# Output projection block by block, plain operands in other rows, x1 stored in halves: one change to a hybrid decoder block on one core

## The chip, the core and the metric

The kernel runs on one core of a Trainium2 chip. Time is device time in microseconds (us) of one execution. The profile is one execution recorded by the hardware profiler, and its engines are PE (TensorE, matmuls; PEld its weight loads), DVE (VectorE), ACT (ScalarE), POOL (GpSimd) and SP (SyncE, which here only issues DMAs). "PEclk" is the share of full speed that the throttle granted to TensorE.

## The reference

A decoder block on x of 1024 tokens by 1024 channels, fp32: an input projection, two token mixers (A: gated chunks, B: dilated windowed attention), and then

```python
gates = jax.nn.sigmoid(gate_logits.reshape(b, s, N_BRANCHES, D_MODEL))
merged = gates[:, :, 0] * (y_a @ w_branch_a[layer]) + gates[:, :, 1] * (y_b @ w_branch_b[layer])
x = x + merged @ w_out[layer]
h2 = rms_norm(x, ffn_norm_g[layer])
up = h2 @ w_up[layer]
a, val = up[..., :D_FF], up[..., D_FF:]
a = causal_depthwise_conv(a, conv_w[layer], conv_b[layer])
x = x + (jax.nn.gelu(a, approximate=False) * val) @ w_down[layer]
```

and a final RMSNorm. D_FF is 2816, handled as 22 units of 128 columns (`ff` = 0 to 21). The change touches the span from the gating of the last branch tiles to the first units of `h2 @ w_up`.

## The kernel before

**Products.** Every large product is a 2x2 Strassen-Winograd scheme: seven products P1 to P7 of half-size operands with sums before and after them. Each is done in three passes of rounded fp32 parts (hi by hi, hi by lo, lo by hi). `to_parts` makes an operand: ACT copies the source into the hi part (L165), DVE or POOL subtracts it from the source for the lo part (L166). A 128x512 output tile is one bank of PSUM; three pools hold them: `acc` (3 banks), `dn` (3 banks) and `tr` (2 banks).

**What sets the order.** PE follows the order of the program throughout. From `write_order()` on, during the last branch tiles, until the last product of unit 1 (P3), DVE and ACT follow the order of the program too; the order is written out by hand there, down to single operations: `to_parts` puts its lo subtraction on a list, and `low(n)` emits the next n of them. POOL and SP, and what the program makes behind that stretch, go where a scheduler puts them, and a tile's buffer or row of SBUF can be reused once all its readers are done.

**Branch merge** (L1205, L1304 to L1309). Per channel tile `dt` and token half `h`, PE makes `pa` and `pb`, ACT takes the sigmoid of the gates `g` (L1304; for `dt` 6 and 7 just before the use), and DVE multiplies and adds. `pa` sits in an `acc` bank, `pb` in a `dn` bank.

**Output projection** (`out_step`, L1555; `out_result`; the large loop over `OSEQ`). The products come in the order P1, P2, P6, P5, P3, P7, P4, each of four token blocks `blk` and four contraction tiles `kt`, so 12 matmuls of 512 columns a block. P2 adds into the banks of P1, P3 into those of P5, P4 into those of P7. Blocks 0 to 2 of P1 and P5 are in `acc` banks, block 3 in a `tr` bank. P1 runs `kt` outermost: the first tile of all four blocks, then the second. The other products run block by block. `out_ops` are the operands from `w_out` (`out_op`), the first three in a tile called `lead`. After a block of P3 (tokens 0 to 511) or P4 (tokens 512 to 1023) its 1024 channels are complete: ACT squares and sums the last half (`square_h`, L1503), SP stores the row block to `x1d` in DRAM (in `norm_h`, L1511, 512 KB), POOL makes the scale in three small operations (`finish_rms`, L2023 and L2028), ACT and DVE scale a half each (`scale_h`, L1516 and L1517), PE transposes (`turn_h`, L1462), and DVE writes the transposed block over the old one in `Y` (L1466). So L1466 must wait until the store of that block has read `Y`.

**Beginning of the up projection** (`beginning_up`). Unit 0 is a plain product in four pieces (`plain_product_up`, `pu`, L1701) with operands `plain_up[which, k]` in the rows R13, R14, R15 and opx0 of SBUF. They are made at P4: `(0,0)` and `(0,1)` of `up_0_0` ahead of P4's first block, `(1,0)` and `(1,1)` of `up_1_0` behind its first two blocks. Units 1 and 2 run as `up_product` (L1722): P1 and P2 of unit 1, P1 and P2 of unit 2, then the second tokens' half of the plain unit (`pu_1_0`, `pu_1_1`), then P6, P7, P5, P4, P3 of unit 1. ACT copies P1 out (`t1`, L1735) before P2 may add into the same bank; P4 adds into the bank of P7 after DVE has read it (`v`, L1743). `sums_h` (L1816 to L1819) makes the sums of the second operand on DVE, `taps` (L1657 on ACT, then L1659 on DVE) the convolution. In between DVE makes the lows of the operands A21, A22, S2, S3, S1, S4.

The lines that matter most for the change:

```python
if name == "P1":
    out_step(accs[m], name, s, m)
else:
    out_step(accs[n], name, 4 * j + m, n)
...
plain_rows = {(0, 0): (R, 13), (0, 1): (R, 14), (1, 0): (R, 15), (1, 1): (opx, 0)}
lead_rows = {(1, "P1"): (opx, 1), (1, "P2"): (opx, 2), (2, "P1"): (opx, 3), (2, "P2"): (R, 12)}
```

## Time and profile before

| | |
|---|---|
| median of three runs | 1428.24 us (1427.3 to 1428.31) |
| the profiled execution's own time | 1428.74 us |
| its span | 1427.0 us |
| PE busy | 1392.2 us, 98% of the span |
| DVE, ACT, POOL busy | 71%, 46%, 21% |
| mean granted clock | 0.991 |

The span has four large stages by the lines that PE runs: the input projection and attention to about 585 us, the branch merge to 673 us, the output projection from there to 765 us, the up projection to about 1200 us, and the down projection to the end. The change lies between 660 and 830 us. A row of the timeline gives the start, the duration, the engine, the line and the tiles (out<-in), and in brackets how long the engine had been idle before it and whose result it waited for. A row of windows gives, for a stretch of time, the busy time of each engine, the granted clock and the share of the DMA engines.

### The profile page before, as it was taken

The page shows a single profiled execution, that of the slowest core. Times are in us where ns is not written, and L with a number is a line of the kernel's source. Part 1 is how long each engine was busy: PE and PEld are TensorE (multiplying, and loading weights), DVE is VectorE, ACT ScalarE, POOL GpSimd, SP SyncE. Part 2 cuts the span into 40 slices and gives each one's busy share as a digit, 9 for nine tenths or more (in the row PEclk, how much of TensorE's full clock was granted, in tenths as well). Part 3 has the DMA queues.
Part 4 walks back from the last instruction along what each step waited for, and adds up shares of the span by engine and source line. Part 5 has one row for each costly group of instructions (what it writes and reads, how often), then busy time and mean ns, then how long its engine had stood idle before and what let it go on. Part 6 is the DMA issues. An engine that isn't in the chain of part 4 may idle for free.

```text
span 1427.0 us, 19428 instructions
## 1 busy us (share of the span) xinstructions
PE 1392.2 (98%) x6534; PEld 1149.2 (81%) x6534; DVE 1007.8 (71%) x1887; ACT 650.9 (46%) x1266; POOL 298.7 (21%) x296
## 2 busy tenths in 40 slices
PE   8899999999999999999999899999999999999997
PEld 7777788888888888887887678888888887888886
DVE  7877677676886987768787866556556557676674
ACT  5554255555553333533545533333333435354453
POOL 0002000000231000111001165555655543000002
PEclk9999999999999999999999999999999999999999
DMA  6013636354435996793742122223333227986663
GB/s 238 15 48 104 192 85 181 98 175 133 134 111 192 338 311 226 231 300 117 250 150 96 45 103 90 80 89 118 119 119 117 85 95 242 360 317 240 199 205 118
DMA packets 140340, 230.73 MB, mean 162 GB/s; under 512 B 13392, under 2 KB 57168, under 8 KB 140240
## 3 DMA queue, kind: packets, MB, share of 16 engines
q1 hardware_dynamic: 138800, 227.33, 47.9%
q10 hardware_dynamic: 1440, 2.16, 0.4%
q8 instruction: 51, 0.84, 0.2%
q14 instruction: 49, 0.40, 0.1%
HBM read 163.57 MB, written 64.29 MB: 160 GB/s over the span
## 4 chain that ended last, share of the span: by engine, by line
PE 83%; DVE 9%; issue 3%; ACT 2%; POOL 1%; DMA 1%; SPq 0%; POOLq 0%; DVEq 0%; ACTq 0%
PE in_P L491 27%; PE uP L1722 19%; PE dn L1923 12%; PE up L1722 7%; PE wo_P L1555 4%; PE pa L1205 3%; PE pu L833 2%; PE pl L552 2%; DVE R L166 1%; PE pp L817 1%; PE pb L1205 1%; PE warm L344 1%; PE sc L778 1%; PE sc L779 1%; DVE G L166 1%
## 5 line engine op out<-in xcount | busy, mean ns | idle before, releaser
L491 PE MATMUL in_P<-R,G 128*128 128x512 f32 x1008 | 243.7, 394 | 0.0
L491 PEld LDWEIGHTS in_P<-R,G 128*128 128x128 f32 x1008 | 185.6, 188 | 36.8
L1923 PE MATMUL dn<-R 128*128 128x512 f32 x924 | 209.6, 389 | 0.0
L1923 PEld LDWEIGHTS dn<-R 128*128 128x128 f32 x924 | 173.4, 188 | 36.0
L1722 PE MATMUL uP<-R,opx 128*128 128x512 f32 x756 | 183.6, 396 | 0.6 <-POOL opx L166 0.6
L1722 PEld LDWEIGHTS uP<-R,opx 128*128 128x128 f32 x756 | 142.6, 189 | 34.7 <-POOL opx L166 1.0
L165 ACT ACTIVATE G<-wr 128x512 fp32r<-128x512 f32 x126 | 79.1, 630 | 151.2 <-PE in_P L491 114.9
L1722 PE MATMUL uP<-G,opx 128*128 128x512 f32 x504 | 126.7, 401 | 5.2 <-DVE Y L1743 4.8
L491 PE MATMUL in_P<-G,G 128*128 128x512 f32 x504 | 122.7, 394 | 1.0 <-DVE C L518 1.0
L1722 PEld LDWEIGHTS uP<-G,opx 128*128 128x128 f32 x504 | 96.3, 192 | 28.8 <-issue 3.6
L165 ACT ACTIVATE opx<-up 128x512 fp32r<-128x512 f32 x88 | 55.5, 632 | 130.6 <-DVE up L278 55.7
L1722 PE MATMUL up<-G,R 128*128 128x512 f32 x468 | 113.1, 390 | 0.7 <-ACT t L1735 0.7
L491 PEld LDWEIGHTS in_P<-G,G 128*128 128x128 f32 x504 | 92.8, 188 | 19.8 <-ACT G L165 1.2
L1722 PEld LDWEIGHTS up<-G,R 128*128 128x128 f32 x468 | 87.9, 188 | 20.1 <-ACT t L1735 1.1
L166 DVE TENSOR_TENSOR G<-wr,G 128x512 fp32r<-128x512 f32 x126 | 87.8, 698 | 21.7 <-ACT G L165 21.6
L165 ACT ACTIVATE R<-db 128x512 fp32r<-128x512 f32 x77 | 48.3, 629 | 68.1 <-PE dn L1923 53.8
L166 DVE TENSOR_TENSOR R<-db,R 128x512 fp32r<-128x512 f32 x77 | 53.7, 701 | 27.9 <-ACT R L165 27.8
L491 PE MATMUL in_P<-G 128*128 128x512 f32 x252 | 62.2, 393 | 0.0
L884 POOL TENSOR_TENSOR ld<-ld,w 128x256 f32<-128x256 f32 x16 | 11.2, 721 | 236.5 <-DVE w L872 236.5
L1751 POOL TENSOR_TENSOR Y<-Y 128x512 f32<-128x512 f32 x21 | 32.2, 1534 | 132.7 <-ACT Y L1654 132.7
L166 POOL TENSOR_TENSOR wbl<-wbs,wbh 128x512 fp32r<-128x512 f32 x12 | 16.0, 1348 | 199.9 <-DMA gated<-C 139.0
L166 POOL TENSOR_TENSOR opx<-up,opx 128x512 fp32r<-128x512 f32 x40 | 56.7, 1417 | 0.0
(283 smaller groups left out, 2516.4 us busy)
## 6 DMA issues: line engine op xcount, KB each, us to landing
wr<-in_w_in_dram SPq DMA_DIRECT2D x46, 512.0 KB, 4.0
up<-in_w_up_dram SPq DMA_DIRECT2D x44, 512.0 KB, 4.2
dA<-gd SPq DMA_DIRECT2D x55, 256.0 KB, 5.0
wd<-in_w_down_dram SPq DMA_DIRECT2D x44, 256.0 KB, 5.2
wT<-wd SPq DMA_DIRECT2D x44, 256.0 KB, 4.0
dS<-gS SPq DMA_DIRECT2D x44, 256.0 KB, 4.2
db<-wT SPq DMA_DIRECT2D x44, 256.0 KB, 4.6
gd<-Y SPq DMA_DIRECT2D x42, 256.0 KB, 2.0
```

What stands on the lines that cost most here:

```text
L165: nc.scalar.activation(hi, src, AF.Copy)
L166: fn = lambda: lo_eng.tensor_tensor(lo, src, f32(hi), ALU.subtract)
L344: nc.tensor.matmul(warm[:, :P], ident, ident, start=True, stop=True)
L491: nc.tensor.matmul(acc, op[:, w, kt, :], left[LEFT[name], kt][:, a, :], start=opened and kt == 0 and i == 0, stop=kt == QK - 1 and i == 2, ...
L552: nc.tensor.matmul(acc, plain_ops[n, k, i][:, w, kt, :], left[f"A{h + 1}{k + 1}", kt][:, a, :], start=k == 0 and kt == 0 and p == 0, stop= ...
L778: nc.tensor.matmul(dst, self.qa[:, h, :], keys, start=True, stop=False)
L833: nc.tensor.matmul(pu[:, h * HD : (h + 1) * HD], self.pT[:, i, :], vt[:, h * HD : (h + 1) * HD], start=i % n == 0, stop=i % n == n - 1,)
L1205: nc.tensor.matmul(acc, unit[a][kt // 4][:, kt % 4, :], two(R, 8 * h + kt)[:, b, :], start=n == 0 and i == 0, stop=n == len(kts) - 1 and i ...
L1555: nc.tensor.matmul(acc, left[LEFT[name], kt][:, a, blk * P : (blk + 1) * P], out_ops[s][:, w, :], start=name not in SHARED and kt == 0 and ...
L1722: nc.tensor.matmul(acc, op[:, w, kt, :], left[LEFT[name], kt][:, a, :], start=opened and kt == 0 and i == 0, stop=kt == QK - 1 and i == 2, ...
L1751: nc.gpsimd.tensor_tensor(ge1, ge1, v, ALU.mult)
L1923: nc.tensor.matmul(accs[blk], dops[s][:, 0, a, blk * P : (blk + 1) * P], dops[s][:, 1, w, :], start=SEQ[j] not in CONTINUES and kt == 0 an ...
```

## The change

1. **P1 of the output projection runs block by block** like the others. Its first three blocks are copied out (L1523, ACT) after the third block, the fourth after itself.
2. **Gates.** `gate_b` is split: `gate_load` issues the two loads, `sigmoid` the activation. For `dt` 6 and 7 each stands on its own line now, the sigmoid one product or more ahead of the `merge` that uses it; the sums, the operands of `w_out` (`out_op`) and the lows between the last four merges are reordered.
3. **The plain unit's operands** move to the rows R4 to R7 and are made behind blocks 2 and 3 of P7. Their sources are loaded from the end of P3. Their lows stand behind the first result of P4.
4. **x1 is stored in halves**: `square_h` stores the half that it squares (256 KB), `norm_h` stores nothing. For the blocks 4 to 7 the transposed lower half goes to `s3` (a part of the tile `own`) instead of over the old one, and `sums_h`, A21 and S3 read it there.
5. **Leads regrouped**: P1 of unit 1, P1 of unit 2, P2 of unit 1, P2 of unit 2, for the making of operands and on PE.
6. **Taps split** into `begin_taps` (ACT) and `end_taps` (DVE), with other work of the two engines between them; S3's parts are made ahead of the taps of units 1 and 2, and `pu_1_1` runs ahead of the making of S1's parts.

How the instructions stand, at three places (`wo_P7_1` is the PSUM bank of P7 and P4, block 1; the trailing number only tells one tile from another). PE at the beginning of the first product, before:

```order
L1555 MATMUL wo_P1_0_6169<-lead_5423,G0_77 128x512 x3
L1555 MATMUL wo_P1_1_6170<-lead_5423,G0_77 128x512 x3
L1555 MATMUL wo_P1_2_6171<-lead_5423,G0_77 128x512 x3
L1555 MATMUL wo_P1_3_6172<-lead_5423,G0_77 128x512 x3
L1555 MATMUL wo_P1_0_6169<-lead_5423,G0_77 128x512 x3
```

and after the change:

```order
L1565 MATMUL wo_P1_0_6169<-lead_5423,G0_77 128x512 x9
L1565 MATMUL wo_P1_0_6169<-R_75,G0_77 128x512 x3
L1565 MATMUL wo_P1_1_6170<-lead_5423,G0_77 128x512 x9
L1565 MATMUL wo_P1_1_6170<-R_75,G0_77 128x512 x3
L1565 MATMUL wo_P1_2_6171<-lead_5423,G0_77 128x512 x9
```

The bank of block 2 is first written after 6 matmuls before, and after 24 now; the fourth operand (`R_75`) is first read after 36 matmuls before, and after 9 now.

DVE around the end of P7 and the beginning of P4, before (L1541 adds P7's result, L1546 P4's; the `up_` rows are the lows of the plain unit's operands; L1517 scales, L1466 writes the transposed halves):

```order
L1541 TENSOR_TENSOR Y_5416<-Y_5416,wo_P7_3_6609 128x512
L166 TENSOR_TENSOR R_75<-up_0_0_6684,R_75 128x512 x2
L1546 TENSOR_TENSOR Y_5416<-Y_5416,wo_P7_0_6606 128x512
L166 TENSOR_TENSOR R_75<-up_1_0_6686,R_75 128x512
L1546 TENSOR_TENSOR Y_5416<-Y_5416,wo_P7_1_6607 128x512
L1517 TENSOR_SCALAR xn_4_1_6772<-Y_5416,fr_n2_4_6748 128x512
L1466 TENSOR_TENSOR Y_5416<-ht_4_0_6789,chan_80 128x512
L1466 TENSOR_TENSOR Y_5416<-ht_4_1_6795,chan_80 128x512
```

and after the change (L1551, L1556, L1527 and L1475 are the same lines by their new numbers):

```order
L1551 TENSOR_TENSOR Y_5416<-Y_5416,wo_P7_3_6617 128x512
L1556 TENSOR_TENSOR Y_5416<-Y_5416,wo_P7_0_6614 128x512
L166 TENSOR_TENSOR R_75<-up_0_0_6610,R_75 128x512 x2
L1556 TENSOR_TENSOR Y_5416<-Y_5416,wo_P7_1_6615 128x512
L1527 TENSOR_SCALAR xn_4_1_6780<-Y_5416,fr_n2_4_6762 128x512
L166 TENSOR_TENSOR R_75<-up_1_0_6612,R_75 128x512
L1475 TENSOR_TENSOR own_6241<-ht_4_0_6797,chan_80 128x512
L1475 TENSOR_TENSOR Y_5416<-ht_4_1_6803,chan_80 128x512
```

The first result of P4 stands ahead of the two lows of `up_0_0` now, and the first low of `up_1_0` behind the scaling of block 4; the lower transposed half goes to `own`.

ACT from the scaling of block 7 on, before (the four rows `R_75<-Y_5416` are the hi parts of A21, `G1_76<-Y_5416` those of A22, then of S2; `t1` is the copy of a P1):

```order
L1516 ACTIVATE xn_7_0_6884<-Y_5416,fr_n2_7_6854 128x512
L165 ACTIVATE R_75<-Y_5416 128x512 x4
L1657 ACTIVATE own_6241<-pu_0_0_6857,chan_80 128x512
L165 ACTIVATE G1_76<-Y_5416 128x512 x4
L1826 ACT_TABLE_LOAD
L1826 ACTIVATE own_6241<-own_6241 128x512
L165 ACTIVATE opx_6155<-up_0_2_6752 128x512
L165 ACTIVATE R_75<-up_0_2_6752 128x512
L1735 ACTIVATE t1_1_6980<-up_1_6967 128x512
L1735 ACTIVATE t1_2_7017<-up_2_7004 128x512
L165 ACTIVATE G1_76<-Y_5416 128x512 x4
L1657 ACTIVATE Y_5416<-up_1_6967,chan_80 128x512
```

and after the change:

```order
L1526 ACTIVATE xn_7_0_6892<-Y_5416,fr_n2_7_6862 128x512
L165 ACTIVATE R_75<-up_0_3_7175 128x512
L165 ACTIVATE R_75<-own_6241 128x512 x4
L1663 ACTIVATE own_6241<-pu_0_0_6865,chan_80 128x512
L165 ACTIVATE G1_76<-Y_5416 128x512 x4
L1835 ACT_TABLE_LOAD
L1835 ACTIVATE own_6241<-own_6241 128x512
L165 ACTIVATE opx_6155<-up_0_1_6694 128x512
L165 ACTIVATE R_75<-up_0_2_6716 128x512
L1743 ACTIVATE t1_1_6988<-up_1_6975 128x512
L1743 ACTIVATE t1_2_7003<-up_2_6990 128x512
L165 ACTIVATE G1_76<-Y_5416 128x512 x4
```

The hi part of unit 3's P2 operand, from `up_0_3`, stands directly behind the scaling of block 7 and ahead of A21's parts; before, the same operation came 15 rows further down. Its lo part has moved likewise on DVE, from behind the first result of unit 1's P6 to ahead of the transposed block 7. No line of the diff says so: the program makes this operand behind the stretch written out by hand, the scheduler may put it ahead, and the row R14 that it writes no longer holds an operand of the plain unit. It waits for the load of `up_0_3`, which in turn waits for the second low of `up_1_0`, whose buffer it takes.

The diff, cut to its core (the reordered calls of the merges are shown by their first half):

```diff
+    def gate_load(dt, h):
+        t = gates[dt, h] = wp.tile([P, 2, HALF], F32, name=f"g_{dt}_{h}", tag="gt", bufs=3)
+        for br in range(2):
+            nc.sync.dma_start(t[:, br, :], gated[br, dt, :, h * HALF : (h + 1) * HALF])
+    def sigmoid(dt, h):
+        nc.scalar.activation(gates[dt, h], gates[dt, h], AF.Sigmoid)
     def gate_b(dt):
-        if dt < KT:
-            for h in range(2) if dt < KT - 1 else (1, 0):
-                t = wp.tile([P, 2, HALF], F32, name=f"g_{dt}_{h}", tag="gt", bufs=3)
-                for br in range(2):
-                    nc.sync.dma_start(t[:, br, :], gated[br, dt, :, h * HALF : (h + 1) * HALF])
-                if dt < LAST_B:
-                    nc.scalar.activation(t, t, AF.Sigmoid)
-                gates[dt, h] = t
+        for h in range(2):
+            gate_load(dt, h)
+            if dt < LAST_B:
+                sigmoid(dt, h)
...
         gt = gates[dt, h]
-        if dt >= LAST_B:
-            nc.scalar.activation(gt, gt, AF.Sigmoid)
         nc.vector.tensor_tensor(gt[:, 0, :], gt[:, 0, :], pa, ALU.mult)
...
     last_b = write_order()
-    sums_and_parts(1)
     prep_b(KT - 1)
+    sigmoid(KT - 2, 0)
     for q in range(2):
...
         out_load(q, st.rearrange("p (k a) c -> p k (a c)", k=2))
+    gate_load(KT - 1, 1)
+    sums_and_parts(1)
+    out_op(0)
+    out_op(1)
+    sigmoid(KT - 2, 1)
+    low(1)
     mm = merge_mm(KT - 2, 0)
-    low(1)
     merge(KT - 2, 0, *mm)
-    gate_b(KT - 1)
-    out_op(0)
-    low(1)
-    out_op(1)
-    low(1)
+    gate_load(KT - 1, 0)
+    low(3)
+    out_op(2)
+    sigmoid(KT - 1, 1)
     mm = merge_mm(KT - 2, 1)
-    low(1)
     merge(KT - 2, 1, *mm)
-    out_op(2)
...
-    plain_rows = {(0, 0): (R, 13), (0, 1): (R, 14), (1, 0): (R, 15), (1, 1): (opx, 0)}
+    plain_rows = {(0, 0): (R, 4), (0, 1): (R, 5), (1, 0): (R, 6), (1, 1): (R, 7)}
     lead_rows = {(1, "P1"): (opx, 1), (1, "P2"): (opx, 2), (2, "P1"): (opx, 3), (2, "P2"): (R, 12)}
...
-    order = [(1, "P1"), (1, "P2"), (2, "P1"), (2, "P2")]
+    order = [(1, "P1"), (2, "P1"), (1, "P2"), (2, "P2")]
     order += [(1, name) for name in ("P6", "P7", "P5", "P4", "P3")]
...
             gain = chan[:, GAIN + 4 * c : GAIN + 4 * c + 4]
+            dst = Y[:, b, c * HALF : (c + 1) * HALF] if c or b < 4 else s3[:, b - 4, :]
             nc.vector.tensor_tensor(
-                Y[:, b, c * HALF : (c + 1) * HALF].rearrange("p (k t) -> p k t", k=4),
+                dst.rearrange("p (k t) -> p k t", k=4),
                 pt.rearrange("p (k t) -> p k t", k=4),
...
             sqs2[b] = small.tile([P, 2], F32, name=f"sq_{b}", tag="sq", bufs=8)
+        cs = slice(c * HALF, (c + 1) * HALF)
+        nc.sync.dma_start(x1_t[:, b, cs], Y[:, b, cs])
         nc.scalar.activation(
...
-        nc.sync.dma_start(x1_t[:, b, :], Y[:, b, :])
         scales[b] = finish_rms(nc, small, mhalf, sqs2[b], f"n2_{b}")
...
     TURNS = {18: 0, 19: 1, 20: 2, 21: 3, 26: 4, 27: 5}
-    LOWS = {21: 2, 22: 4, 23: 4, 24: 2, 25: 1, 26: 1, 27: 0}
+    BEFORE = {21: 2, 22: 4, 23: 4, 24: 0, 25: 0, 26: 0, 27: 0}
+    AFTER = {20: 2, 24: 2, 25: 1, 26: 1}
     for kt in range(4):
...
         out_banks[name] = accs
-        if name == "P4":
-            plain_up_op(0, 0)
-            plain_up_op(0, 1)
         for n in range(4):
...
                     turn_h(TURNS[s], acc_tile)
-                if name == "P1":
-                    out_step(accs[m], name, s, m)
-                else:
-                    out_step(accs[n], name, 4 * j + m, n)
+                out_step(accs[n], name, 4 * j + m, n)
                 if m % 2 == 1:
                     tick()
-            low(LOWS.get(s, 9))
+            low(BEFORE.get(s, 9))
             if name == "P1":
+                for blk in range(3) if n == 2 else range(n, n + n // 3):
+                    out_result(name, blk, accs[blk])
                 if n == 3:
-                    for blk in range(4):
-                        out_result(name, blk, accs[blk])
                     own = leadp.tile([P, 6, HALF], F32, name="own", tag="lead")
...
                 residual(1, 0, 3)
-            if s == 20:
-                low(2)
-            elif n == 3 and j < 5:
+            if n == 3 and j < 5:
                 low(9)
-            if name == "P7" and n == 1:
+            if s == 19:
                 up_load(0, 0)
                 up_load(0, 1)
-            if name == "P4":
-                up_ahead(5, 0)
-                if n < 2:
-                    plain_up_op(1, n)
-                elif n == 3:
-                    up_ahead(7, 1)
+            elif s in (21, 22):
+                up_ahead(1 if s == 21 else 5, 0)
+            if s in (22, 23):
+                plain_up_op(s - 22, 0)
+                plain_up_op(s - 22, 1)
+            low(AFTER.get(s, 0))
+            if s == 27:
+                up_ahead(7, 1)
     spare = [s3[:, i, :] for i in range(3)]
...
-        taps(cv, src, ff, edge)
+        begin_taps(cv, src, ff)
+        end_taps(cv, src, ff, edge)
         nc.scalar.activation(cv, cv, AF.Gelu)
-    def taps(cv, src, ff, edge):
+    def begin_taps(cv, src, ff):
         nc.scalar.activation(cv, src, AF.Identity, bias=cw(3, ff), scale=cw(2, ff))
+    def end_taps(cv, src, ff, edge):
         for j, o in ((1, 1), (0, 2)):
...
         tt, sub = nc.vector.tensor_tensor, ALU.subtract
-        a11, a12, a21, a22 = (Y[:, b - 4 + 4 * i, half] for i in range(2) for half in (lower, upper))
+        a11, a12, a22 = Y[:, b - 4, lower], Y[:, b - 4, upper], Y[:, b, upper]
+        a21, total = s3[:, b - 4, :], Y[:, b, lower]
         return (
-            lambda: tt(s3[:, b - 4, :], a11, a21, sub),
-            lambda: tt(a21, a21, a22, ALU.add),
-            lambda: tt(a11, a21, a11, sub),
+            lambda: tt(total, a21, a22, ALU.add),
+            lambda: tt(a21, a11, a21, sub),
+            lambda: tt(a11, total, a11, sub),
             lambda: tt(a12, a12, a11, sub),
...
         })
-        left_parts(UP_ROWS, "A21", Y[:, 4:8], 0)
+        left_parts(UP_ROWS, "A21", s3, 0)
+        begin_taps(ge_of(0, 0), gate0, 0)
         low(4)
         keep_edge(0, gate0)
-        taps(ge_of(0, 0), gate0, 0, None)
+        end_taps(ge_of(0, 0), gate0, 0, None)
         value0 = plain_product_up(0, 1, {})
...
         up_product(1, "P1")
-        for fn in (q4, p5, r4, q5, p6, r5, q6, p7, r6, q7):
+        up_product(2, "P1")
+        for fn in (q4, p5, r4, q5, p6, r5, q6, p7, r6, q7, s4, r7):
             fn()
         up_product(1, "P2")
-        up_product(2, "P1")
-        s4()
-        r7()
         left_parts(UP_ROWS, "S2", Y[:, 0:4], 0)
...
         low(4)
+        left_parts(UP_ROWS, "S3", s3, 0)
+        for ff in (1, 2):
+            begin_taps(ge_of(ff, 0), banks[ff, "P2"], ff)
+        up_ahead(9, 5)
         for ff in (1, 2):
             keep_edge(ff, banks[ff, "P2"])
-            taps(ge_of(ff, 0), banks[ff, "P2"], ff, None)
-        left_parts(UP_ROWS, "S3", s3, 0)
+            end_taps(ge_of(ff, 0), banks[ff, "P2"], ff, None)
         for ff in (1, 2):
             gelu(ge_of(ff, 0))
-        up_ahead(9, 5)
         low(5)
         gate1 = plain_product_up(1, 0, {})
-        taps(ge_of(0, 1), gate1, 0, edges.pop(0))
+        begin_taps(ge_of(0, 1), gate1, 0)
         up_ahead(9, 6)
+        end_taps(ge_of(0, 1), gate1, 0, edges.pop(0))
+        value1 = plain_product_up(1, 1, {})
+        low(1)
         left_parts(UP_ROWS, "S1", Y[:, 4:8], 0)
-        value1 = plain_product_up(1, 1, {})
         gelu(ge_of(0, 1))
-        low(5)
+        low(4)
         up_ahead(9, 7)
```

More of the change, by code (lines that the diff above doesn't have):

```diff
@@ L1358, in block_kernel @@
     mix_part("S2", 2)
+    sigmoid(KT - 1, 0)
+    mm = merge_mm(KT - 1, 1)
+    merge(KT - 1, 1, *mm)
     s4()
     low(1)
-    mm = merge_mm(KT - 1, 1)
-    merge(KT - 1, 1, *mm)
     out_op(3)
     low(1)
-    for kt in range(3):
-        mix_part("S4", kt)
-        low(1)
+    mix_part("S4", 0)
+    low(1)
+    mix_part("S4", 1)
     mm = merge_mm(KT - 1, 0)
     merge(KT - 1, 0, *mm)
-    low(1)
+    mix_part("S4", 2)
+    low(2)
     s1, s3, s2, s4 = mix_sums(3)
     s1()
+    mix_part("S1", 3)
     s3()
@@ L1375, in block_kernel @@
     s2()
-    mix_part("S1", 3)
     mix_part("S2", 3)
+    low(1)
     s4()
```

1 line of the change is left out of this document (added).

## The prediction

> **What bounds the kernel now.** The page first: busy times, and the chain that ended last.
>
> ```profile
> PE 1392.2 (98%) x6534; PEld 1149.2 (81%) x6534; DVE 1007.8 (71%) x1887; ACT 650.9 (46%) x1266; POOL 298.7 (21%) x296
> PE 83%; DVE 9%; issue 3%; ACT 2%; POOL 1%; DMA 1%; SPq 0%; POOLq 0%; DVEq 0%; ACTq 0%
> ```
>
> TensorE is the bound. The diff changes no matmul, so it can gain only where PE stands idle or runs at a lower clock. Next the windows over the changed stretch (busy time of PE, PEld, DVE, ACT, POOL, then granted clock, DMA share, GB/s):
>
> ```profile
> 673.40:745.00 71.60, 68.24 (x310) 55.15 (x310) 55.57 (x91) 36.53 (x72) 4.05 (x12) 1.00 0.57 195
> 745.00:765.00 20.00, 17.23 (x77) 13.82 (x76) 13.65 (x23) 10.19 (x23) 3.40 (x9) 0.91 0.46 139
> 765.00:800.00 35.00, 33.63 (x154) 27.11 (x153) 31.03 (x53) 19.32 (x34) 2.30 (x4) 1.00 0.09 34
> 800.00:830.00 30.00, 25.85 (x97) 19.62 (x96) 25.86 (x41) 14.75 (x26) 10.16 (x8) 0.89 0.20 70
> ```
>
> PE idles 3.4, 2.8, 1.4 and 4.2 us in them, 11.7 us in all, and the clock falls in two: 0.09 of 20 us is 1.8 us lost, 0.11 of 30 us up to 3.3 us. So about 17 us is to be had here. DVE is full from 765 to 800 (31.0 of 35 us). Then PE's timeline for the single waits:
>
> ```profile
> 677.98 7.24 PE L1555 MATMUL wo_P<-lead,G 128*128 128x512 f32 x30 [2.97 <-DVE g L1305]
> ...
> 736.47 0.63 PE L1462 MATMUL ht<-ident,xn 128*128 128x128 f32 x4 [0.39 <-DVE xn L1517]
> ...
> 757.45 1.09 PE L1462 MATMUL ht<-ident,xn 128*128 128x128 f32 x8 [2.77 <-ACT xn L1516]
> 758.30 1.19 PE L1555 MATMUL wo_P<-opx,G 128*128 128x512 f32 x3
> 759.29 1.48 PE L1555 MATMUL wo_P<-R,G 128*128 128x512 f32 x3
> ...
> 764.29 0.85 PE L1555 MATMUL wo_P<-R,G 128*128 128x512 f32 x3
> ...
> 781.43 5.87 PE L1722 MATMUL up<-G,opx 128*128 128x512 f32 x24 [0.69 <-ACT t L1735]
> 787.98 3.01 PE L1722 MATMUL up<-G,R 128*128 128x512 f32 x12 [0.69 <-ACT t L1735]
> ...
> 802.82 2.58 PE L1722 MATMUL uP<-G,opx 128*128 128x512 f32 x10 [0.41 <-DVE opx L166]
> ...
> 814.36 5.46 PE L1722 MATMUL uP<-G,opx 128*128 128x512 f32 x12 [3.16 <-DVE Y L1743]
> ...
> 822.70 2.96 PE L1722 MATMUL uP<-G,opx 128*128 128x512 f32 x12
> ...
> 829.49 5.39 PE L1722 MATMUL uP<-R,opx 128*128 128x512 f32 x22 [0.58 <-POOL opx L166]
> ```
>
> Three waits are near 3 us. The first is for a PSUM bank, the second for a normalised row block, the third for the eviction that P4 of unit 1 needs. Behind the second and the third PE runs slow (three matmuls take 1.48 us against 0.85, twelve 5.46 against 2.96); behind the first, at clock 1.00, it does not.
>
> **The change, part by part**, against this execution (1428.74 us by its own time, 0.50 above the median, 1427.0 of it the span).
>
> *a. First product and gates.* These rows are the sigmoid and the multiplication that frees the bank:
>
> ```profile
> 676.17 1.04 ACT L1304 ACTIVATE g<-g 128x1024 f32<-128x1024 f32 x1
> ...
> 677.24 0.69 DVE L1305 TENSOR_TENSOR g<-g,pa 128x512 f32<-128x512 f32 x1 [0.52 <-ACT g L1304]
> ```
>
> Block order writes block 2's bank after 24 matmuls instead of 6. Thirty took 7.24 us (row 677.98), so 0.24 each: the bank is wanted 18 x 0.24 = 4.3 us later, at 675.0 + 4.3 = 679.3, and it was free at 677.9. The sigmoid issued early frees it sooner still. Two edits cover one stall, so only one is paid: **-3.0**. The fourth operand is read sooner, after 9 matmuls instead of 36; ACT is without the 1.04 us sigmoid in front of it then, and its making is moved ahead by two merges. P2's operands could be late next; by ACT's and DVE's order they come about 1 us ahead, so 0 to +1, taken as 0.
>
> *b. x1 in halves.* DVE's write of the transposed block waits for the store to have read `Y`:
>
> ```profile
> 733.44 1.29 DVE L1466 TENSOR_TENSOR Y<-ht,chan 128x512 f32<-128x512 f32 x2 [1.71 <-DMA x1d<-Y]
> ...
> x1d<-Y SPq DMA_DIRECT2D x8, 512.0 KB, 4.2
> ...
> gd<-own SPq DMA_DIRECT2D x2, 256.0 KB, 2.0
> ```
>
> A store of half the size took 2.0 us against 4.2, and the first half leaves earlier. The wait of 1.71 is gone, and with it PE's 0.39 at 736.47, which is DVE's lateness from here: **-0.4** (0 if the second half lands as late). SP issues 8 more DMAs; its queue has room (DMA share 0.46 and 0.09 above), so nothing for that. [...]
>
> *c. Block 4's chain.* DVE and ACT, in order, ahead of the wait at 757.45:
>
> ```profile
> 750.22 0.68 DVE L1541 TENSOR_TENSOR Y<-Y,wo_P 128x512 f32<-128x512 f32 x1
> 751.62 1.14 ACT L165 ACTIVATE R<-up 128x512 fp32r<-128x512 f32 x2
> 752.27 1.30 DVE L166 TENSOR_TENSOR R<-up,R 128x512 fp32r<-128x512 f32 x2 [1.37 <-ACT R L165]
> 753.49 0.68 DVE L1546 TENSOR_TENSOR Y<-Y,wo_P 128x512 f32<-128x512 f32 x1
> ...
> 754.26 0.63 ACT L1503 ACTIVATE own<-Y 128x512 bf16<-128x512 f32 x1 [1.50 <-DVE Y L1546]
> ...
> 755.71 0.92 POOL L2028 TENSOR_TENSOR fr_n<-fm_n,mhalf 128x1 f32<-128x1 f32 x1
> ...
> 756.67 0.72 ACT L1516 ACTIVATE xn<-Y,fr_n 128x512 f32<-128x512 f32 x1 [1.17 <-POOL fr_n L2028]
> ```
>
> L1546 stood behind the two lows, which waited 1.37 us for ACT. Now it follows L1541 at once, at about 750.9, 2.6 us sooner. ACT still has the square of block 7's upper half and two hi copies (751.62) ahead of this block's square, until 752.8, so the square starts 754.26 - 752.8 = 1.4 to 1.5 sooner; and no operand copy stands between the square and the scaling any more. I take the scaled block 1.75 sooner (between 1.4 and 2.6): the wait goes from 2.77 to 1.0. Half-clock matmuls follow a wait of 2.77 here and none of those of 0.69 or less; at 1.0 I take full clock, so the 1.8 us go too: **-3.5** (-1.4 to -4.6).
>
> *d. DVE's chain to P4 of unit 1.* From block 7's transposition on, PE asks for DVE's `v` (L1743) and DVE is the slower:
>
> ```profile
> 769.98 1.29 DVE L1466 TENSOR_TENSOR Y<-ht,chan 128x512 f32<-128x512 f32 x2
> ...
> 774.79 1.53 DVE L1659 SCALAR_TENSOR_TENSOR own<-pu,chan,own 128x511 f32<-128x511 f32 x2 [0.85 <-ACT own L1657]
> ...
> 793.72 1.54 DVE L1659 SCALAR_TENSOR_TENSOR Y<-up,chan,Y 128x511 f32<-128x511 f32 x2 [0.90 <-ACT Y L1657]
> ...
> 796.04 2.18 ACT L165 ACTIVATE R<-own 128x512 fp32r<-128x512 f32 x4
> 796.17 1.53 DVE L1659 SCALAR_TENSOR_TENSOR Y<-up,chan,Y 128x511 f32<-128x511 f32 x2 [0.85 <-ACT Y L1657]
> ...
> 809.67 0.69 DVE L166 TENSOR_TENSOR R<-up,R 128x512 fp32r<-128x512 f32 x1
> ...
> 813.53 0.68 DVE L1743 TENSOR_TENSOR Y<-Y,uP 128x512 f32<-128x512 f32 x1
> ```
>
> From 769.98 to 813.53 are 43.55 us, of which 0.85 + 0.90 + 0.85 = 2.6 are waits for the first tap on ACT. The split puts that tap ahead, under other lows, so all three go. The same operations remain. Unit 3's low (809.67) moves ahead of block 7: it costs its 0.7 us earlier and saves it later, nothing for `v`. So `v` comes **-2.6** relative to block 7. PE's own waits in between (0.69, 0.69, 0.41) must not be counted again: regrouping hides the two copies of P1 behind another product of about 2.9 us, so PE asks 1.4 sooner and still waits, 3.16 - (2.6 - 1.4) = 2.0, or some tenths more if the waits of P6 and P5 grow.
>
> *e. Clock behind that wait.* Twelve matmuls took 5.46 against 2.96, 2.5 lost in the first twelve, at most 3.3 in the window. If 2.0 us of idling leaves the clock up: **-2.6**. If not, 0. [...]
>
> *f. What comes late next.* PE arrives at unit 2's P7 with POOL's low still unfinished:
>
> ```profile
> 828.15 1.28 POOL L166 TENSOR_TENSOR opx<-t,opx 128x512 fp32r<-128x512 f32 x1
> ```
>
> PE waited 0.58 for the next POOL low; running 2.6 us ahead of before it waits longer, though POOL's chain also starts sooner. I take **+0.6** (0 to +2.6) for that and for P3 of unit 1, which waits for P5's eviction when nothing slows PE.
>
> Moving the plain operands costs nothing by itself: ACT and DVE make as many as before, now under P7, when DVE waits for PE. What they leave free, the hoisted operand of unit 3, makes ACT and DVE wait for a load that ACT queues A21 behind; POOL has none of it. Before, such loads took 3.8 to 4.2 us:
>
> ```profile
> 761.11 0.33 SPq L1403 DMA_DIRECT2D up<-in_w_up_dram  x1
> up<-in_w_up_dram SPq DMA_DIRECT2D x9, 512.0 KB, 3.8
> ```
>
> The low that frees its buffer stands ahead of block 5's transposition now, so with c I expect the load some 3 us sooner than 761.11; it lands by 762, and DVE's write of block 7 was at 769.98. That leaves some 3 us ahead of ACT's copy, when this too comes 3.5 sooner. Cost 0.
>
> Sum: 3.0 + 0.4 + 3.5 + 2.6 + 2.6 - 0.6 = **11.5** us. 1428.74 - 11.5 = 1417.2 for a profiled execution; 1428.24 - 11.5 = **1416.7** for the median.
>
> **The rivals.**
>
> *A. Forecast.* All of the above. Own range 1414.7 to 1418.2: 1414.7 if P4's wait of 2.0 goes too, 1418.2 if c yields 2.0.
>
> *B. Half clock stays behind P4 of unit 1.* For it: a wait of 2.77 did it. Against: P4's wait is now about 2, and 2.97 passed once. Without e, and without the +0.6 that e brings: 3.0 + 0.4 + 3.5 + 2.6 = 9.5, so 1418.7.
>
> *C. DVE's chain does not shorten.* For it: the rows of DVE and ACT alternate closely from 765 to 813, and a tap put ahead can itself wait for a PSUM bank or for S3's four hi copies (2.18 us at 796.04), which stand ahead of it now. Then d and e fail: 3.0 + 0.4 + 3.5 = 6.9, so 1421.3.
>
> *D. Block 4's chain does not shorten*, since ACT's copies move ahead of its square: c gives 0 (wait 2.77, clock half). 11.5 - 3.5 = 8.0, so 1420.2.
>
> *E. The edit on P1 does not do what it says*: PE meets another wait of the same 3 us at the fourth operand or at P2's. Against: ACT loses a sigmoid there. 8.5, so 1419.7.
>
> *F. Slower.* The hoisted hi copy holds ACT, which goes in order, until `up_0_3` has landed; A21's four hi copies, the taps and `t1` stand behind it, and PE stands at `pu_1_0`. It must use up the 3 us of margin and then the whole 11.5, so it decides from a landing 14.5 us later than expected, 18 us after the issue where its kind takes 3.8; the sixteen stores in the same queue would have to hold it up. Landing 18 us later than expected gives 1416.7 + 15 = 1431.7.
>
> **How the numbers follow.** A 0.50, B 0.20, C 0.13, D 0.07, E 0.07, F 0.03. The time is A's, 1416.7. The range holds A, B, D, E and C's 1421.3 with some tenths more: 1414.2 (A's lower end, and c larger by 0.5) to 1421.8. About 0.2% (2.9 us) is what a measurement of this kernel can tell from no change; A to E give 6.9 or more and are all faster. Only a double failure (C with D: 3.4) comes near it, 0.04. So faster 0.93, same 0.04, slower 0.03.
>
> **What would show it.** a: no wait of over 1 us near 675 to 690. c: a wait near 1.0 at block 4's transposition, and PEclk 1.00 in that window. d: DVE without waits for ACT at the taps; 41 us from block 7 to `v`. e: twelve matmuls of P4 in about 2.9 us, and a wait of about 2 ahead of them. b: no waits for stores of x1 at L1466. Wrong would be the forecast if ACT stood idle on `up_0_3` ahead of A21, if P4's wait stayed at 3 us, or if PE idled over 1 us at a place where it did not idle before.

## The result, and the profile after

The changed kernel takes 1417.01 us (median of four runs, 1415.66 to 1417.53) against 1428.28 us: a ratio of 0.9916, 95% interval 0.9898 to 0.9933. Its profiled execution took 1417.45 us, span 1415.7. The forecast was 1416.7.

The windows over the same stretches (busy time of PE, PEld, DVE, ACT, POOL, then granted clock, DMA share, GB/s):

```profile
673.40:745.00 71.60, 71.60 (x327) 58.40 (x326) 57.36 (x94) 36.79 (x75) 4.05 (x12) 1.00 0.65 211
745.00:765.00 20.00, 19.18 (x100) 15.76 (x100) 16.27 (x29) 11.09 (x24) 5.63 (x13) 1.00 0.39 130
765.00:800.00 35.00, 35.00 (x153) 28.21 (x152) 34.51 (x61) 20.14 (x35) 0.00 (x0) 1.00 0.04 16
800.00:830.00 30.00, 25.44 (x102) 19.96 (x101) 21.98 (x30) 12.64 (x23) 18.06 (x13) 0.94 0.33 106
```

PE is full to 800 us but for 0.8 us, at full clock. The last window is as bad as before: 4.6 us idle and a clock of 0.94. PE's timeline has these places:

```profile
673.40 2.26 PE L1565 MATMUL wo_P<-lead,G 128*128 128x512 f32 x9
...
751.58 1.09 PE L1469 MATMUL ht<-ident,xn 128*128 128x128 f32 x8 [0.81 <-ACT xn L1526]
...
753.21 0.85 PE L1565 MATMUL wo_P<-R,G 128*128 128x512 f32 x3
...
770.31 8.53 PE L1730 MATMUL up<-G,opx 128*128 128x512 f32 x36
...
804.22 4.59 PE L1730 MATMUL uP<-G,opx 128*128 128x512 f32 x12 [3.09 <-DVE Y L1751]
808.65 2.96 PE L1730 MATMUL uP<-R,opx 128*128 128x512 f32 x12
...
819.09 5.39 PE L1730 MATMUL uP<-R,opx 128*128 128x512 f32 x22 [1.47 <-POOL opx L166]
...
1192.01 2.33 PE L1730 MATMUL uP<-G,opx 128*128 128x512 f32 x9 [1.28 <-DVE Y L1751]
```

The first product runs without a wait, block 4's transposition waits 0.81 us and three matmuls behind it take 0.85, and the leads run through (36 matmuls in one row). At P4 of unit 1 the wait is still 3.09, twelve matmuls behind it take 4.59 us, and the wait for POOL has grown to 1.47. So not all went as forecast.

Times of whole runs differ by about 2 us for one and the same kernel (1415.66 to 1417.53 after the change, 1414.78 to 1417.69 in e11), and the start of the first product alone lies between 671 and 675 us in the profiles. What an edit does is better read inside a trace. There is one profile of each kernel. I cut each profile at five matmuls: the first of the output projection, the first transposition of block 4, the first matmul of P4 of unit 1, the third of unit 2's P7 (the one that needs POOL's low), and the last. Distances in us, with the median of whole runs beside them:

| kernel | median | to block 4 | to P4 | to unit 2's P7 | to the last | sum |
|---|---|---|---|---|---|---|
| before | 1428.28 | 83.99 | 56.91 | 15.13 | 588.19 | 744.22 |
| after | 1417.01 | 78.19 | 52.64 | 14.87 | 587.79 | 733.48 |
| e1 v first | 1415.96 | 78.21 | 49.41 | 16.90 | 588.19 | 732.71 |
| e2 old lead order | 1418.41 | 78.21 | 52.66 | 14.57 | 589.36 | 734.80 |
| e3 lows first | 1416.75 | 78.32 | 52.66 | 15.14 | 587.81 | 733.93 |
| e4 taps whole | 1420.96 | 78.17 | 56.10 | 14.59 | 589.35 | 738.21 |
| e5 POOL's low sooner | 1414.47 | 78.19 | 52.67 | 13.20 | 587.68 | 731.75 |
| e6 three places | 1414.55 | 78.21 | 49.41 | 15.76 | 587.68 | 731.07 |
| e7 P1 by tile | 1416.68 | 78.19 | 52.68 | 15.11 | 587.88 | 733.87 |
| e8 late gates | 1420.68 | 82.26 | 52.66 | 14.57 | 589.38 | 738.87 |
| e9 and a low on DVE | 1413.28 | 78.19 | 49.40 | 13.62 | 588.20 | 729.41 |
| e10 x1 whole | 1417.44 | 78.51 | 52.68 | 14.97 | 587.87 | 734.03 |
| e11 operands late | 1417.03 | 78.22 | 52.65 | 14.99 | 587.79 | 733.65 |
| e12 and lows first | 1418.94 | 79.83 | 54.24 | 14.60 | 589.37 | 738.05 |

An undisturbed one of the first two distances repeats within 0.05 us from run to run. The change gained 5.80 us up to block 4, 4.27 up to P4, 0.26 up to unit 2's P7 and 0.40 behind it, 10.7 in all; the other 0.55 of the 11.29 by which the profiled span fell lies ahead of the first and behind the last of these matmuls.

### The profile page after: what moved, and what is told of

The parts are those of the page before. It is cut to its first block, busy times and chain, and to the rows that moved or that the text cites. A ratio compares the mean times of both kernels' runs of the same rounds, so it can differ in the third digit from the quotient of the medians.

```text
span 1415.7 us, 19436 instructions
## 1 busy us (share of the span) xinstructions
PE 1387.6 (98%) x6534; PEld 1146.5 (81%) x6534; DVE 1008.1 (71%) x1887; ACT 650.8 (46%) x1266; POOL 299.7 (21%) x296
## 4 chain that ended last, share of the span: by engine, by line
PE 86%; DVE 8%; issue 2%; POOL 2%; ACT 1%; DMA 1%; SPq 0%; POOLq 0%; DVEq 0%; ACTq 0%
PE in_P L491 27%; PE uP L1730 19%; PE dn L1935 12%; PE up L1730 7%; PE pa L1209 5%; PE wo_P L1565 4%; PE pu L833 2%; PE pl L552 2%; PE pb L1209 2%; PE pp L817 1%; DVE G L166 1%; DVE R L166 1%; PE sc L778 1%; PE sc L779 1%; PE warm L344 1%
## 5 line engine op out<-in xcount | busy, mean ns | idle before, releaser
L1759 POOL TENSOR_TENSOR Y<-Y 128x512 f32<-128x512 f32 x21 | 33.6, 1599 | 130.9 <-ACT Y L1660 130.9
```

Of the source, the lines that this page charges most:

```text
L1759: nc.gpsimd.tensor_tensor(ge1, ge1, v, ALU.mult)
```

## The experiments

All are the changed kernel with the edit shown; P3 to P7 without a unit are those of unit 1.

**e1: v first.**

```diff
         left_parts(UP_ROWS, "S4", Y[:, 0:4], 1)
-        low(5)
```

> The changed kernel with one call taken out: the lows of unit 1's P4 operand and of S4 are no longer emitted ahead of unit 1's P7 but behind its eviction v, so v stands 3 us sooner in DVE's queue. Theory (P4 of unit 1 waits only because v is queued behind five lows on DVE): PE's wait of 3.09 us there falls below 0.5 us and the half clock behind it, 0.8 to 1.0 us, goes; POOL's wait of 1.47 us at unit 2's P7 stays about as it is, since POOL's chain starts from P4's result and moves with it. 1417.0 - 2.8 - 0.9 = 1413.3 us. Rival (something else is late right behind it: P4's own operand, S4's lows for P3, or POOL): the wait moves to P3 or to unit 2's P7, and the time stays at 1416 to 1417 us.

Measured 1415.96 us (ratio to before 0.9913, 0.9899 to 0.9927). PE goes on at P4 without a wait, 3.2 us sooner (49.41 against 52.64), but then:

```profile
805.23 4.59 PE L1730 MATMUL uP<-R,opx 128*128 128x512 f32 x12 [2.42 <-ACT opx L165]
...
816.54 5.38 PE L1730 MATMUL uP<-R,opx 128*128 128x512 f32 x22 [0.69 <-POOL opx L166]
```

The wait moved to P3, as the rival had it, with half clock behind it. P3 adds into P5's bank, and DVE's eviction of P5 is the row that ends there; the lows and sums stood ahead of it now:

```profile
803.07 0.68 DVE L277 TENSOR_TENSOR up<-up,up 128x512 f32<-128x512 f32 x1
803.79 0.69 DVE L278 TENSOR_TENSOR up<-up 128x512 f32<-128x512 f32 x1
804.40 0.68 DVE L1755 TENSOR_TENSOR Y<-Y,uP 128x512 f32<-128x512 f32 x1
```

It ends at 805.08, 0.15 before P3 begins. The row of PE names a copy on ACT that ended at about the same time. e6 settles it: there the eviction is moved ahead, P3 starts at 803.79 without a wait, and those copies on ACT come only at 805.68. Of 3.2 us, 2.0 were lost again by unit 2's P7 (16.90 against 14.87).

**e2: old lead order.**

```diff
-    order = [(1, "P1"), (2, "P1"), (1, "P2"), (2, "P2")]
+    order = [(1, "P1"), (1, "P2"), (2, "P1"), (2, "P2")]
...
         up_product(1, "P1")
-        up_product(2, "P1")
...
         up_product(1, "P2")
+        up_product(2, "P1")
```

> The changed kernel with the leads in the old order (P1 and P2 of unit 1, then P1 and P2 of unit 2). Theory (from block 7 to P4 of unit 1 DVE's chain sets the end, so PE's waits in between are paid out of the wait at P4): the two waits for the copy of P1, 0.69 us each in the row and 0.9 from start to start, come back, the wait at P4 shrinks from 3.09 by the same 1.4 to 1.9 us, and the time is 1417.0 us within 0.5, or 0.8 less if the shorter wait leaves the clock up. Rival (the two waits add to the time): 1417.0 + 1.9 = 1418.9 us with the wait at P4 still near 3.

Measured 1418.41 us (ratio 0.9930, 0.9917 to 0.9944).

```profile
774.41 5.84 PE L1730 MATMUL up<-G,opx 128*128 128x512 f32 x24 [0.69 <-ACT t L1743]
780.93 3.01 PE L1730 MATMUL up<-G,R 128*128 128x512 f32 x12 [0.69 <-ACT t L1743]
...
804.70 3.03 PE L1730 MATMUL uP<-G,opx 128*128 128x512 f32 x12 [1.50 <-DVE Y L1751]
...
819.28 4.14 PE L1730 MATMUL uP<-R,opx 128*128 128x512 f32 x10 [2.43 <-POOL opx L166]
```

The distance to P4 is that of the changed kernel (52.66 against 52.64): PE's two waits are paid out of the one at P4, and the regrouping by itself gains nothing there. That is the theory. But the shorter wait left the clock up (1.00 from 802.80 to 809.60), PE came to unit 2's P7 at the same time as POOL's low allowed (14.57), having waited 2.43 there, and half clock followed that wait instead: 1.57 us more to the last matmul. Neither of the two figures expected holds, though the theory on the wait does.

**e3: lows first.**

```diff
-    BEFORE = {21: 2, 22: 4, 23: 4, 24: 0, 25: 0, 26: 0, 27: 0}
-    AFTER = {20: 2, 24: 2, 25: 1, 26: 1}
+    BEFORE = {21: 2, 22: 4, 23: 4, 24: 2, 25: 0, 26: 0, 27: 0}
+    AFTER = {20: 2, 25: 1, 26: 1}
```

> The changed kernel with the two lows of up_0_0 ahead of P4's first result on DVE again. Theory (the place of that result on DVE is what shortened block 4's chain): DVE adds P4's first result 1.2 us later, PE's wait at block 4's transposition grows from 0.81 to about 2.0 us, DVE's chain behind it and so the whole kernel is 1.2 us later, 1418.2 us, and 1.7 us more, 1419.9 us, if a wait of 2.0 halves the clock. Rival (ACT's copies ahead of the square, or POOL's scale, set the chain): the wait stays near 0.8 and the time at 1417.0 us.

Measured 1416.75 us (ratio 0.9919, 0.9906 to 0.9933), no change; the wait at block 4 is 0.97 against 0.81. The rival holds: with the copies already made on ACT, the lows no longer wait, and ACT's work ahead of block 4's square hides them.

**e4: taps whole.**

```diff
         left_parts(UP_ROWS, "A21", s3, 0)
-        begin_taps(ge_of(0, 0), gate0, 0)
         low(4)
         keep_edge(0, gate0)
+        begin_taps(ge_of(0, 0), gate0, 0)
...
-        for ff in (1, 2):
-            begin_taps(ge_of(ff, 0), banks[ff, "P2"], ff)
         up_ahead(9, 5)
         for ff in (1, 2):
             keep_edge(ff, banks[ff, "P2"])
+            begin_taps(ge_of(ff, 0), banks[ff, "P2"], ff)
             end_taps(ge_of(ff, 0), banks[ff, "P2"], ff, None)
```

> The changed kernel with the first tap directly ahead of the others again, for the taps of units 0 to 2 in the first half. Theory (DVE's three waits for ACT's first tap, 2.6 us before, lay on the chain to v): DVE waits 0.85 us three times, v comes 2.6 us later, PE's wait at P4 of unit 1 grows from 3.09 to about 5.7 us; 1417.0 + 2.6 = 1419.6 us, and up to 1 us more if the clock stays halved for longer. Rival (DVE has slack there): the waits come back and the time stays at 1417.0 us.

Measured 1420.96 us (ratio 0.9948, 0.9936 to 0.9960), 3.9 slower than the changed kernel. DVE's waits are back:

```profile
766.89 1.53 DVE L1667 SCALAR_TENSOR_TENSOR own<-pu,chan,own 128x511 f32<-128x511 f32 x2 [0.85 <-ACT own L1663]
788.27 1.53 DVE L1667 SCALAR_TENSOR_TENSOR Y<-up,chan,Y 128x511 f32<-128x511 f32 x2 [1.30 <-ACT Y L1663]
790.72 1.53 DVE L1667 SCALAR_TENSOR_TENSOR Y<-up,chan,Y 128x511 f32<-128x511 f32 x2 [0.85 <-ACT Y L1663]
```

They are 3.0 us, and P4 starts 3.46 us later. The theory holds: DVE has no slack there. PE's wait does not stand at P4 alone, as expected, but is split: 3.29 at P6 for a low of DVE and 1.81 at P4. The rest is again half clock behind POOL's wait (eleven matmuls in 4.15 us; 589.35).

**e5: POOL's low sooner.**

```diff
-        up_ahead(i + 9, i + 4)
+        up_ahead(i + 9, i + 5 if i == 7 else i + 4)
         up_product(ff, name)
```

> The changed kernel with unit 2's P7 operand made one product sooner, so that its hi copy on ACT and its low on POOL stand ahead of the gelu of unit 1's P4 and of the two multiplications on POOL. Theory (from v on, the chain P4, c21, taps, gelu, two POOL multiplications, POOL low sets when PE goes on at unit 2's P7, and swallows the half clock behind P4): PE's wait of 1.47 us there goes, and the time is 1417.0 - 1.5 = 1415.5 us. Rival (POOL has that low late for its own load, not for its place in the queue, or P4's own result is what counts next): the wait moves by less than 0.5 us and the time stays at 1417.0 us.

Measured 1414.47 us (ratio 0.9903, 0.9889 to 0.9918), 2.5 better than the changed kernel in the medians and 1.7 by the distances: the theory's 1.5 and a little more. PE still waits 3.09 at P4, but goes through unit 2's P7 without a wait: 13.20 against 14.87.

**e6: three places.**

```diff
-        left_parts(UP_ROWS, "S4", Y[:, 0:4], 1)
-        low(5)
...
-        up_ahead(i + 9, i + 4)
+        if i > 6:
+            up_ahead(i + 9, i + 5 if i == 7 else i + 4)
         up_product(ff, name)
-        if written[0]:
+        if i == 5:
+            low(1)
+            up_ahead(14, 9)
+            left_parts(UP_ROWS, "S4", Y[:, 0:4], 1)
+        elif i == 6:
+            low(5)
+            up_ahead(15, 10)
+        if written[0] and i != 5:
             low(9)
```

> The changed kernel with three places moved: v ahead of S4's lows on DVE, P5's eviction ahead of them too (without that PE waited 2.42 us at P3 when v alone was moved), and unit 2's P7 operand one product sooner on ACT and POOL. Theory (three waits on one chain, each behind the other): the waits at P4 (3.09), P3 and unit 2's P7 (1.47) all fall below 0.5 us and the half clock behind P4 (0.8 to 1.0) goes; 1417.0 - 2.8 - 1.4 - 0.9 = 1411.9 us. Rival (DVE is simply full up to P3, so that S4's lows or the sums of unit 2 are late instead): a wait of 1 to 3 us appears at P3 of unit 1 or P6 of unit 2, and the time is 1414 to 1416 us.

Measured 1414.55 us (ratio 0.9902, 0.9887 to 0.9916), no better than e5. The rival holds: P4 and P3 go without a wait, and the next late thing is a low of unit 2's P6.

```profile
809.39 4.07 PE L1730 MATMUL uP<-G,opx 128*128 128x512 f32 x10 [1.70 <-POOL opx L166]
```

**e7: P1 by tile.**

```diff
-                out_step(accs[n], name, 4 * j + m, n)
+                if name == "P1":
+                    out_step(accs[m], name, s, m)
+                else:
+                    out_step(accs[n], name, 4 * j + m, n)
...
-                for blk in range(3) if n == 2 else range(n, n + n // 3):
+                for blk in range(4) if n == 3 else ():
```

> The changed kernel with the first product of the output projection by contraction tile again and its four results copied out at its end, the sigmoids still early. Theory (two edits cover one stall, the early sigmoid alone frees the bank in time): the bank of block 2 is free at about 674 and wanted at 674.8, so PE waits less than 0.3 us there, and the time stays at 1417.0 us. Rival (block order is what removed the wait): 3 us come back, 1420 us.

Measured 1416.68 us (ratio 0.9921, 0.9907 to 0.9936). The first 36 matmuls stand in one row:

```profile
673.23 8.55 PE L1565 MATMUL wo_P<-lead,G 128*128 128x512 f32 x36
```

No wait: the early sigmoid is enough by itself, and block order adds nothing to it.

**e8: late gates.**

```diff
+        if dt >= LAST_B:
+            sigmoid(dt, h)
         nc.vector.tensor_tensor(gt[:, 0, :], gt[:, 0, :], pa, ALU.mult)
...
-    sigmoid(KT - 2, 0)
...
-    sigmoid(KT - 2, 1)
...
-    sigmoid(KT - 1, 1)
...
-    sigmoid(KT - 1, 0)
```

> The changed kernel with the sigmoids of the last two channel tiles directly ahead of their merges again, the first product block by block. Theory (block order alone covers it): the bank is free at about 678 and wanted at 679, no wait, and the time stays at 1417.0 us; P2's operands come up to 1 us later on ACT, so 0 to +1. Rival (the early sigmoid is what removed the wait): 2 to 3 us come back, 1419 to 1420 us.

Measured 1420.68 us (ratio 0.9945, 0.9929 to 0.9962), 3.7 slower than the changed kernel.

```profile
685.32 4.16 PE L1563 MATMUL wo_P<-R,G 128*128 128x512 f32 x9 [1.76 <-ACT Y L1531]
```

The wait at P1's bank is indeed gone, but one of 1.76 us appears at P2's first block, which adds into P1's bank and waits for ACT to copy it out; nine matmuls behind it take 4.16 us instead of the 2.26 of nine at full clock (the row at 673.40 above). The distance to block 4 grows by 4.07; the medians differ by less, and in this profile the first product starts 1.3 us sooner than after the change. The rival holds: block order alone moves the wait, it does not remove it.

**e9: and a low on DVE.** e6, and:

```diff
-        lo_eng = nc.vector if name in ("P2", "P5", "P4") or (ff < 3 and name == "P1") else free
+        lo_eng = nc.vector if name in ("P2", "P5", "P4") or (ff, name) == (2, "P6") or (ff < 3 and name == "P1") else free
```

> The kernel of the three moved places (v, P5's eviction, unit 2's P7 operand), and the low of unit 2's P6 operand made on DVE instead of POOL. In that kernel PE waited 1.70 us for this low, which stood on POOL behind another unit's sum, and ran at half clock for 3.4 us behind it. Theory: both go, 1.9 + 1.6; 1414.55 - 3.5 = 1411.1 us, with no wait over 0.6 us from 760 to 1100. Rival (DVE is full: the low and the two sums ahead of it push c21 and the taps back, and the multiplications and lows behind them on POOL are late for unit 2's P7): a wait of 1 to 2 us stays, 1412.5 to 1414.5 us.

Measured 1413.28 us (ratio 0.9892, 0.9879 to 0.9905), the best of all, 3.7 us below the changed kernel and 1.1% below the one before. Time and wait are the rival's (a wait of 1.10 stays), but not its place: PE waits at unit 2's P6 for the very low that was moved, and not at P7.

```profile
810.13 2.59 PE L1730 MATMUL uP<-G,opx 128*128 128x512 f32 x10 [1.10 <-DVE opx L166]
...
800.00:830.00 30.00, 28.32 (x119) 21.90 (x119) 28.14 (x36) 14.86 (x26) 17.90 (x12) 1.00 0.35 113
```

DVE is at 28.1 of 30 us in this window, so it has little time left there. The clock is 1.00 there.

**e10: x1 whole.**

```diff
-        nc.sync.dma_start(x1_t[:, b, cs], Y[:, b, cs])
...
+        nc.sync.dma_start(x1_t[:, b, :], Y[:, b, :])
         scales[b] = finish_rms(nc, small, mhalf, sqs2[b], f"n2_{b}")
```

> The changed kernel with x1 stored a whole row block at a time again, behind both squares; the lower transposed half of blocks 4 to 7 still goes to its own tile. Theory (the whole store, 2.6 to 5.2 us in the trace before, holds DVE's write of the transposed block; halves took 2.0 to 4.1): the waits for stores come back on DVE at blocks 1 to 3 and at the upper half of block 4, PE's 0.4 to 0.6 us at block 2 returns and up to 0.5 more at block 5 or 6; 1417.0 + 0.6 = 1417.6 us. Rival (the own tile for the lower half is what matters, the halving is not): no wait, 1417.0 us.

Measured 1417.44 us (ratio 0.9918, 0.9906 to 0.9931), which the times can't tell from 1417.01. In the trace one of the waits is back, and the distance to block 4 is 0.32 longer:

```profile
728.50 1.29 DVE L1475 TENSOR_TENSOR Y<-ht,chan 128x512 f32<-128x512 f32 x2 [1.44 <-DMA x1d<-Y]
```

**e11: operands late.** Lows still behind P4's first result.

```diff
-            if s in (22, 23):
-                plain_up_op(s - 22, 0)
-                plain_up_op(s - 22, 1)
+            if s in (23, 24):
+                plain_up_op(s - 23, 0)
+                plain_up_op(s - 23, 1)
```

> The changed kernel with the four operands of the plain unit made one step later, so that ACT has the two hi copies of up_0_0 between block 7's square and block 4's, as before the change; their lows still stand behind P4's first result on DVE. Theory (either is enough: the result ahead of the lows, or the copies made sooner): PE's wait at block 4 stays at 0.8 to 1.1 us, and the time at 1417.0 us. Rival (the copies made sooner are what shortened the chain): the wait is 2 us or more, and the time 1418.5 to 1420.5 us.

Measured 1417.03 us (ratio 0.9914, 0.9901 to 0.9927), the wait at block 4 0.82: the theory. DVE waits 0.78 us for ACT's copies as before the change, but the result stands ahead of that.

**e12: and lows first.** e11 and e3 together.

> The same with the two lows of up_0_0 ahead of P4's first result on DVE as well, which is the arrangement before the change. Theory: now the lows wait for ACT's copies and the result for the lows, PE's wait at block 4 returns to about 2.8 us, two more than after the change, and half clock may follow; 1417.0 + 2.0 = 1419.0 us, or 1420.6 with the half clock. Rival (another part of the change, such as the lower half's own tile, shortened the chain): the wait stays under 1.2 us, and the time at 1417.0 us.

Measured 1418.94 us (ratio 0.9930, 0.9918 to 0.9943). This is the median of five executions, 1417.86 to 1420.63; a sixth took 3133.84 us, is left out and not explained.

```profile
746.37 1.30 DVE L166 TENSOR_TENSOR R<-up,R 128x512 fp32r<-128x512 f32 x2 [1.37 <-ACT R L165]
747.59 1.28 DVE L1556 TENSOR_TENSOR Y<-Y,wo_P 128x512 f32<-128x512 f32 x2
...
751.17 1.09 PE L1469 MATMUL ht<-ident,xn 128*128 128x128 f32 x8 [2.38 <-ACT xn L1526]
...
752.98 1.48 PE L1565 MATMUL wo_P<-R,G 128*128 128x512 f32 x3
```

The chain of before is back whole: the lows wait 1.37, the wait at block 4 is 2.38, half clock follows. It costs 1.64 up to block 4 and 1.60 up to P4, 3.2 us together. The medians of whole runs are only 1.9 apart: in this profile the first product starts 2.1 us sooner than after the change, and half clock behind POOL's wait adds 1.6 at the end (589.37).

## Why the prediction was right, and where it was not

The sum came out (11.5 us forecast, 11.3 in the medians), but not every term: e failed, and several small ones made up for it by luck. By one of the forecast's own signs, P4's wait staying at 3 us, it was wrong at that place.

**a, forecast 3.0: right in size, wrong in its reason.** The wait is gone without another in its place, and the second product starts 3.2 us sooner after the first. But "two edits cover one stall" was wrong. e7 shows that the sigmoid alone does it. e8 shows that block order alone does not: PE waits 1.76 us at P2's first block instead, and the clock halves (0.51 from 685.77 to 689.19). That block order takes the wait from P1's own bank was worked out rightly; that P1's copies then stand on ACT behind operands that the late sigmoids had delayed was not seen.

**b, forecast 0.4.** From block 2's transposition to block 3's PE takes 0.6 us less than before. The store's part of that is 0.3 by e10; what gave the rest no run shows. The halves took 2.0 to 4.25 us, 3.0 at the median, not the 2.0 taken from another store of that size. The shortest half took 2.0 us and the shortest whole store before 2.6, so a halved size did not halve the time. If the time grew evenly with the size, these two stores (2.0, less the 0.6 between them) would leave 1.4 us that does not depend on it; that is an estimate from the two alone. The own tile for the lower half took away two waits of DVE (1.97 at block 4, 1.34 at block 5), but up to block 7 PE gained nothing by it: from block 4's transposition to block 7's it took 11.8 us before and 11.9 in e12, which has the own tile and the same half clock.

**c, forecast 3.5.** The wait went from 2.77 to 0.81 (1.0 forecast), and the half clock went. e12 puts the whole chain at 3.2 us. e3 and e11 add that two edits cover it, and either would do: the operands made sooner, or the result ahead of the lows. The prediction rested it mainly on the second.

**d, forecast 2.6 for v.** The three waits on ACT are gone. From block 7's transposition to v are 40.42 us now, against 43.55:

```profile
762.98 0.68 DVE L1475 TENSOR_TENSOR own<-ht,chan 128x512 f32<-128x512 f32 x1
...
800.38 0.69 DVE L166 TENSOR_TENSOR opx<-up,opx 128x512 fp32r<-128x512 f32 x1 [0.70 <-ACT opx L165]
800.99 2.49 DVE L166 TENSOR_TENSOR R<-Y,R 128x512 fp32r<-128x512 f32 x4
803.40 0.68 DVE L1751 TENSOR_TENSOR Y<-Y,uP 128x512 f32<-128x512 f32 x1
```

The gain itself came: of the 4.27 us up to P4, 1.6 is c's half clock (e12), which leaves 2.7. e4 puts the split at 3.5 us, and e2 shows that PE's own waits in between must not be counted again. What failed is the wait that remains: 2.0 forecast, 3.09 measured. I took PE's waits by their idle time, 0.69 each; from start to start each copy of P1 had cost 0.85 more than a running matmul, and the 0.41 at P6, which I kept, went too. So PE asked for v as much sooner as v came. The hoisted low was taken to cost v nothing; it costs some 0.4 us. Ahead of block 7 it holds DVE up (DVE writes block 7 7.0 us sooner than before, PE is 7.4 sooner at that point), and where it had stood it leaves a hole: DVE waits 0.70 at 800.38 for a copy that the low had covered.

**e, forecast 2.6: failed.** The step took it that a wait of 2.0 would leave the clock up and that this would be gained whole. Both were my estimates, and no run shows the 2.6. The wait was 3.09, half clock came (rival B; 0.50 from 805.07 to 808.48), and yet the time is not B's. Of shorter waits, 1.50 (e2) and 1.81 (e4) at P4 left the clock up, and 1.70 at unit 2's P6 (e6), 2.38 at block 4 (e12) and 2.42 at P3 (e1) did not. The step's other half was wrong as well: this half clock costs little in either kernel. With 6.8 us of it P4 to unit 2's P7 takes 15.1 us (before, e3), with 3.4 us 14.9 (after), with none 14.6 (e2, e4): 0.5 us between all and nothing. What ends that stretch is a chain over other engines. Here is the chain of waits of the changed kernel there:

```profile
804.22 4.60 PE uP L1730 x12
808.83 0.02 issue
808.85 0.69 DVE Y L1757
809.54 1.53 DVE opx L166
811.07 1.77 DVE Y L1667
...
813.86 0.37 ACT Y L1660
...
816.08 1.74 POOL Y L1763
817.82 1.23 POOL opx L166
819.05 0.04 issue
819.09 5.39 PE uP L1730 x22
```

Behind P4's result come another operand's low, the convolution, a gelu (L1660) and two multiplications (L1759 and L1763), and behind all these on POOL the low that PE wants.

**f, forecast 0.6 against us.** The wait grew from 0.58 to 1.47. It is the other side of e, not a term beside it. e5 shows it: with that low ahead of the multiplications the stretch falls to 13.2 us.

**What made up for e.** Of the 1.7 us by which e less f fell short (2.0 forecast, 0.26 measured), 0.65 came back from a to c up to block 4 (5.80 against 5.15 without the clock), where each was a little larger than forecast. Another 0.40 came behind unit 2's P7, most of it from a wait near the end of the up projection that was 1.65 us before and 1.28 after:

```profile
1202.81 3.03 PE L1722 MATMUL uP<-G,opx 128*128 128x512 f32 x12 [1.65 <-DVE Y L1743]
```

In e1 it is 1.65 again. The last 0.55 lies outside the five matmuls, 0.49 of it behind the last one, where 9.35 us became 8.86; in e10 it is 9.30. The diff has no line at either place, and neither saving is there in every run with the change, so I count these 0.95 us as luck.

The rival on the hoisted load had no part: ACT copied at 761.21, 1.9 us after the load had landed at 759.31 (3 forecast), and A21's copies waited for DVE, not for it.

```profile
761.21 0.61 ACT L165 ACTIVATE R<-up 128x512 fp32r<-128x512 f32 x1
763.70 2.20 ACT L165 ACTIVATE R<-own 128x512 fp32r<-128x512 f32 x4 [1.88 <-DVE own L1475]
```

## What to carry to other kernels

Where a second engine's chain ends the stretch, PE's waits and slow matmuls inside it are not terms of a sum: cost the chain from end to end, and ask what its last link is queued behind. Of two edits that seem to cover the same wait, undo each alone; one may do nothing and the other everything. When a wait goes, look one step further along the same bank and the same queue, as the wait moved from P4 to P3 to the next unit's operand in e1, e6 and e9.
